# A feed-forward stage in Winograd form: who forms the sums, and in which order the engines' instructions stand

## The chip, the cores and the metric

The program runs on one core of one Trainium2 chip. Its metric is the device time of one execution in microseconds (us). Work is done by five engines, each of which takes its own instructions in their order: TensorE (PE; its weight loads are shown apart as PEld), VectorE (DVE), ScalarE (ACT), GpSimd (POOL) and SyncE (SP). SP issues plain transfers here, POOL issues those that add to what lies at the destination.

## The reference, cut to what matters

Two layers; each is a feed-forward part, a mix of three token mixers, and a second feed-forward part. The change touches the feed-forward parts alone, of which there are four:

```python
def swiglu(h, w_in, w_out):
    gate, up = jnp.split(h @ w_in, 2, axis=-1)
    return (jax.nn.silu(gate) * up) @ w_out
...
    x = x + 0.5 * swiglu(rms_norm(x, ffn1_norm[l]), ffn1_w_in[l], ffn1_w_out[l])
...
    x = x + 0.5 * swiglu(rms_norm(x, ffn2_norm[l]), ffn2_w_in[l], ffn2_w_out[l])
```

x is 512 tokens by 1024 features in float32, w_in 1024 by 5632, w_out 2816 by 1024.

## The kernel before, in words

Every float32 operand is split into a high and a low half of type fp32r (`hi` is a cast on ScalarE, `lo` the difference on VectorE), and a product is three matmuls: high by high, high by low, low by high (`mm3`, lines 214, 218 and 219).

Each feed-forward part has three stretches. The first columns of w_in (six of 22 blocks of 128, four in one part) are multiplied plainly in `cover`, which hides the norm and the preparation of x. The bulk runs in `halved`, a Winograd scheme: a 2-by-2 block product with seven products in place of eight, for which sums of quarters of the weights and of the other operand have to be formed. The last six blocks of w_out are multiplied plainly behind it. The bulk is here called a **stage**; there are four in the trace.

A stage is a list `seq` of products. ("I", w, p) is product p of one unit of w_in (two blocks of columns); ("O", (c, g), p) is product p of one unit of w_out (chunk c of eight hidden blocks, half g). Three stages have 84 products, one has 91. One product is 24 matmuls of 128x256 (two column blocks, four row blocks, three matmuls). While products of later I units run, the O units of the chunk that is complete run between them, in a pattern such as "IIO".

Around each place n of `seq` (here: a **slot**) `halved` emits, through `run(n)`, what later products need:

- `load` (line 568): one quarter of a unit's weights, 512 KB, by an SP transfer into one of eight buffers, four slots before its first use.
- `add` (line 572), `add_second` (line 575) and `add_hidden` (line 623): POOL transfers that add 512 KB from memory, from `S`, or from another quarter of the hidden values `hq`. The sums of an I unit are called S1 (quarter 2 plus quarter 3), S2 (that plus quarter 0), S3 (quarter 0 plus quarter 2) and S4 (quarter 1 plus S2). Before the change S1, S3 and S4 are such transfers, and S2 is a VectorE sum (`second`, line 579). In O units all sums of weights are transfers. The four sums of hidden quarters for each chunk are transfers too.
- `moving` (lines 611 to 620): splits a sum of hidden quarters into halves.
- `prepare` (by `parted`, lines 202 and 203): splits the weights of product n + `LEAD` (2) into a buffer `hl`, of which there are three.

Behind a product come its readings of PSUM: VectorE adds an O product to xT (line 731); for I products ScalarE copies (lines 736, 743, 746) and VectorE adds (739, 749, 752), and the last product of a unit makes hidden values (lines 455, 459, or y in lines 766 to 772).

The order in which the instructions of one engine stand is set by the framework's scheduler, which is free to move an instruction ahead of others that were emitted earlier, as far as dependences allow. `follow` ties an instruction behind the one given to it before on the same engine; before the change only the opening uses it.

Of the kernel before, what the change touches and what calls it, by code (L numbers as in the profile page):

```python
# [32 lines left out]

ORDER_IN = ("P1", "P2", "P6", "P5", "P7", "P3", "P4")
ORDER_OUT = ("P2", "P1", "P5", "P6", "P7", "P3", "P4")
LEAD = 2
# [11 lines left out]
F_Q, F_K, F_V, F_F = 1792, 2304, 2816, 3328  # L48


class Trunk:
# [105 lines left out]
    def act(self, out, in_, func, **kw):  # L157
        i = self.nc.scalar.activation(out, in_, func, **kw)
        if self.tab is not None:
            self.tc.add_manual_dep(i.ins, self.tab, NOSYNC, reason="table order")  # L160
        self.tab_users.append(i.ins.name)

    def follow(self, engine, i):

        if engine in self.chain:
            self.tc.add_manual_dep(i.ins, self.chain[engine], NOSYNC, reason="opening order")
        self.chain[engine] = i.ins.name
# [41 lines left out]
    def mm3(self, acc, ah, al, bh, bl, first, last, parted=False):  # L209

        nc = self.nc
        n = bh.shape[-1]
        for c in (slice(0, n // 2), slice(n // 2, n)) if parted else (slice(0, n),):
            nc.tensor.matmul(  # L214
                acc[:, c], ah, bh[:, c], start=first and c.start == 0, stop=False,
                skip_group_check=True,
            )
        nc.tensor.matmul(acc, ah, bl, start=False, stop=False, skip_group_check=True)  # L218
        nc.tensor.matmul(acc, al, bh, start=False, stop=last, skip_group_check=True)  # L219
# [232 lines left out]
    def hidden(self, out, g, u, other):  # L452

        if other:
            self.nc.vector.scalar_tensor_tensor(
                out=out, in0=g, scalar=-1.0, in1=u, op0=ALU.mult, op1=ALU.mult
            )
        else:
            self.nc.vector.tensor_mul(out, g, u)
# [62 lines left out]
    def halved(self, fp, w_in, w_out, covered):  # L522
# [14 lines left out]
        H = T // 2  # L537

        into = lambda c: [
            ("I", f, p) for f in range(max(covered, c[0]), c[0] + c[1], 2) for p in ORDER_IN  # L540
        ]
        outof = lambda c: [("O", (c, g), p) for p in ORDER_OUT for g in range(2)]
        seq = into(CHUNKS[0])
        for c, pattern in ((0, "IIIO" + "IIO" * 12 + "IO"), (1, "IIIO" + "IOIIO" * 6 + "O")):
            ii, oo = iter(into(CHUNKS[c + 1])), iter(outof(c))
            seq += [next(ii if k == "I" else oo) for k in pattern]
            assert next(ii, None) is None and next(oo, None) is None
        at = {s: n for n, s in enumerate(seq)}

        raw, sums, parts, mov = {}, {}, {}, {}  # L550
        first = covered
        todo = {}

        def when(n, rank, fn, *args):
            todo.setdefault(max(n, -1), []).append((rank, fn, args))

# [9 lines left out]
        def load(u, q, tag):  # L566
            raw[u, q] = t = self.res.tile([P, 4, 2 * P], F32, tag=f"x{tag}", name=self.n("w"))
            nc.sync.dma_start(t, src(u, q))

        def add(u, q, q2):  # L570

            nc.gpsimd.dma_start(raw[u, q], src(u, q2), accum_op=ALU.add)  # L572

        def add_second(u):
            nc.gpsimd.dma_start(raw[u, 1], sums[u], accum_op=ALU.add)

        def second(u):
            sums[u] = t = fp.tile([P, 4, 2 * P], F32, tag="S", name=self.n("S"), bufs=2)
            nc.vector.tensor_add(t, raw[u, 2], raw[u, 0])  # L579

        def at_once(u, name):

            a, b, c, op = {
                1: lambda: (raw[u, 2], raw[u, 2], raw[u, 3], ALU.add),
                3: lambda: (raw[u, 0], sums[u], raw[u, 3], ALU.subtract),
                4: lambda: (raw[u, 1], raw[u, 1], sums[u], ALU.add),
            }[name]()
            nc.vector.tensor_tensor(a, b, c, op=op)

        def prepare(kind, w, p):  # L590
# [9 lines left out]
        SUM = {  # L600
            "P2": (1, 0), "P1": (0, 0), "P5": (0, 0), "P6": (0, 0), "P7": (0, 1),
            "P3": (1, 1), "P4": (0, 0),
        }

        def moving(c, p):
# [5 lines left out]
            if p in ("P1", "P7", "P4"):  # L611
                nc.scalar.activation(hi, t, AF.Copy, scale=-1.0)
                nc.vector.scalar_tensor_tensor(
                    out=lo, in0=t, scalar=-1.0, in1=hi, op0=ALU.mult, op1=ALU.subtract
                )
            else:
                nc.scalar.copy(hi, t)
                nc.vector.tensor_sub(lo, t, hi)
# [6 lines left out]
        lives = []  # L625
        units = list(dict.fromkeys((k, w) for k, w, _ in seq))
        for u in units:
            kind, w = u
            split = {p: at[kind, w, p] - LEAD for p in ORDER_IN}
            if kind == "I":  # L630
                end = {0: "P7", 1: "P3", 2: "P5", 3: "P4"}
                m = split["P6"] - 1
                begin = {
                    0: split["P1"] - AHEAD_LOAD, 1: split["P2"] - AHEAD_LOAD,
                    2: m - AHEAD_SUM - AHEAD_LOAD + 1, 3: split["P4"] - AHEAD_LOAD,
                }
                if w == first:
                    begin = {0: -4, 1: -3, 2: -2, 3: -1}
                    when(0, 0, at_once, u, 1)
                    when(0, 0, second, u)  # L640
                    when(split["P7"] - 1, 2, at_once, u, 3)
                    when(split["P3"] - 1, 2, at_once, u, 4)
                else:
                    when(m - AHEAD_SUM, 5, add, u, 2, 3)
                    when(m, 2, second, u)
                    when(max(m, split["P1"]), 5, add, u, 0, 2)
                    when(max(m, split["P2"]), 6, add_second, u)
            else:
                end = {0: "P7", 1: "P2", 2: "P3", 3: "P4"}
                begin = {  # L650
                    0: split["P1"] - AHEAD_LOAD, 1: split["P2"] - AHEAD_LOAD,
                    2: split["P5"] - AHEAD_SUM - AHEAD_LOAD + 1, 3: split["P4"] - AHEAD_LOAD,
                }
                when(split["P5"] - AHEAD_SUM, 5, add, u, 2, 3)
                when(split["P5"] + 1, 5, add, u, 2, 0)
                when(split["P1"] + 1, 5, add, u, 0, 2)
                when(split["P6"] + 1, 5, add, u, 2, 1)
            for q in range(4):
                lives.append((begin[q], split[end[q]], u, q))

        free = {t: -99 + t for t in range(8)}
        for b, e, u, q in sorted(lives, key=lambda x: x[0]):
            t = min(free, key=free.get)
            assert free[t] <= max(b, 0), (u, q, b, free)
            free[t] = e
            when(b, 4, load, u, q, t)
        for c in range(2):
            n0 = {p: at["O", (c, 0), p] for p in ORDER_OUT}
            for p in ORDER_OUT:
                when(n0[p] - (2 if p == "P2" else 3), 3, moving, c, p)  # L670
            when(n0["P1"] - 2, 7, add_hidden, c, (0, 0), (0, 1))
            when(n0["P5"] - 2, 7, add_hidden, c, (0, 0), (1, 1))
            when(n0["P5"] - 1, 7, add_hidden, c, (0, 1), (1, 1))
            when(n0["P6"] - 2, 7, add_hidden, c, (0, 0), (1, 0))

        def product(u, p, bank, start, stop, parted):
            hi, lo = parts.pop((u, p))
            xh, xl = self.xc[p] if u[0] == "I" else mov[u[1][0], p]
            for i in range(2):
                acc, c = bank[:, i * H : (i + 1) * H], slice(i * P, (i + 1) * P)  # L680
                for k in range(4):
# [3 lines left out]
                        parted and i == 0 and k == 0,  # L685
# [9 lines left out]
        def run(n):  # L695
            if n >= 0 and n + LEAD < len(seq):
                when(n, 1, prepare, *seq[n + LEAD])
            for _, fn, args in sorted(todo.pop(n, []), key=lambda x: x[0]):
                fn(*args)

        run(-1)
        for s in seq[:LEAD]:
            prepare(*s)
        yield
        ring = {"I": (self.ntog + 1) % 2, "O": self.ntog % 2}
# [7 lines left out]
        for n, (kind, w, p) in enumerate(seq):  # L713
            run(n)
# [6 lines left out]
            product(u, p, acc, p in new, p in ("P2", "P3", "P4"), n == 0)  # L721
            if kind == "O":
                c, g = w

                for r, b, f in {
# [5 lines left out]
                    nc.vector.scalar_tensor_tensor(  # L731
                        out=xs, in0=pair(acc), scalar=f, in1=xs, op0=ALU.mult, op1=ALU.add
                    )
            elif p == "P1":
                work[u, "g1"] = g1 = tmp("g1")
                nc.scalar.activation(g1, acc, AF.Copy, scale=-1.0)
            elif p == "P2":
                g1 = work[u, "g1"]
                nc.vector.tensor_add(g1, g1, acc)
                self.act(g1, g1, AF.Silu)  # L740
            elif p == "P6":
                work[u, "g2"] = g2 = tmp("g2")
                nc.scalar.activation(g2, acc, AF.Copy, scale=-1.0)  # L743
            elif p == "P5":
                work[u, "u2"] = u2 = tmp("u2")
                nc.scalar.activation(u2, acc, AF.Copy, scale=-1.0)
            elif p == "P7":
                u2 = work[u, "u2"]
                nc.vector.tensor_add(u2, u2, acc)
            elif p == "P3":  # L750
                g2 = work[u, "g2"]
                nc.vector.tensor_add(g2, g2, acc)
                self.act(g2, g2, AF.Silu)
            else:
                g1, g2, u2 = (work[u, x] for x in ("g1", "g2", "u2"))
                c = next(i for i, (f0, nf) in enumerate(CHUNKS) if f0 <= w < f0 + nf)
                if c < 2:
                    a, k = divmod(w - CHUNKS[c][0], 4)
                    for b, g, v in ((1, g2, u2), (0, g1, acc)):
                        self.hidden(  # L760
                            self.quarter(fp, c, a, b)[:, k : k + 2, :], pair(g), pair(v), a != b
                        )
                else:
                    q = (w - CHUNKS[c][0]) // 2
                    y = fp.tile([P, 2, T], F32, tag="S", name=self.n("y"), bufs=2)
                    nc.vector.tensor_mul(y[:, :, H:], pair(g2), pair(u2))
                    nc.vector.tensor_mul(y[:, :, :H], pair(g1), pair(acc))
# [738 lines left out]
```

## Time and profile before

| | us |
|---|---|
| median of three runs (1947.43 to 1953.0) | 1948.43 |
| profiled execution, its own time | 1955.04 |
| its span, first to last instruction | 1953.3 |
| PE busy in the span | 1875.0 (96%) |
| DVE busy | 1404.8 (72%) |
| ACT busy | 1000.8 (51%) |

The four stages lie at 82.3 to 338.1, 696.6 to 952.6, 1029.7 to 1299.4 and 1657.8 to 1912.4 us of the span; the mixes lie between the first and second and between the third and fourth. In rows that group instructions the first part is line, engine, operation, output and inputs; then the count, the busy time in us, the mean of one in ns, and the idle time of the engine just before them with what ended it. A matmul's busy time overlaps the next one's, so a busy PE need not be at its peak; PEclk is the share of the full clock that was granted.

### The profile page before, as it was taken

What the parts mean: (1) busy time and instruction counts of PE and PEld (TensorE: products, weight loads), DVE (VectorE), ACT (ScalarE), POOL (GpSimd) and SP (SyncE); (2) the same over time, 40 slices, a digit from 0 to 9 for tenths busy, and PEclk for the clock granted to TensorE, in tenths of its full rate; (3) what the DMA queues carried; (4) which work ended last, traced back from release to release, by engine and by line L of the source; (5) the groups of instructions that cost most, each with busy time, mean ns of one, the idle gap of its engine ahead of it and who ended that gap; (6) DMA issues with size and microseconds to landing.
All of it is one profiled execution on the core that took longest, in us unless ns stands there. A gap on an engine that the chain in (4) does not pass through costs nothing.

```text
span 1953.3 us, 33198 instructions
## 1 busy us (share of the span) xinstructions
PE 1875.0 (96%) x13384; PEld 1735.3 (89%) x13384; DVE 1404.8 (72%) x2048; ACT 1000.8 (51%) x1483; POOL 239.8 (12%) x239
## 2 busy tenths in 40 slices
PE   8998999999999998999999989999999999989999
PEld 6898999899878798899989989998998778889997
DVE  7964767578787866677677667766868878756773
ACT  4544455464675543455454545545546663544552
POOL 0022120100000012122001221301000000220310
PEclk9999999999999999999999999999999999999999
DMA  5598794332323389889247989923323234897972
GB/s 140 173 213 176 177 236 106 76 97 71 74 80 103 96 209 198 167 211 220 67 140 169 220 175 213 219 80 76 93 60 88 82 97 144 206 186 180 213 151 87
DMA packets 265658, 281.79 MB, mean 144 GB/s; under 512 B 20608, under 2 KB 246912, under 8 KB 265504
## 3 DMA queue, kind: packets, MB, share of 16 engines
q1 hardware_dynamic: 191792, 183.69, 31.5%
q0 software_dynamic: 73712, 95.97, 30.0%
q8 instruction: 105, 1.72, 0.4%
q14 instruction: 49, 0.40, 0.1%
HBM read 240.23 MB, written 2.10 MB: 124 GB/s over the span
## 4 chain that ended last, share of the span: by engine, by line
PE 67%; DVE 13%; DMA 11%; issue 5%; ACT 4%; POOL 0%; SPq 0%; DVEq 0%; ACTq 0%; POOLq 0%
PE mm L214 10%; PE mm L219 10%; PE mm L218 10%; DMA w<-in_ffn_w_in_dram 7%; DVE hl L203 4%; PE sc L219 4%; PE sc L214 4%; PE sc L218 4%; PE pt L219 4%; PE pt L214 4%; PE pt L218 4%; DMA hq<-hq 3%; PE po L219 3%; PE po L214 2%; PE po L218 2%
## 5 line engine op out<-in xcount | busy, mean ns | idle before, releaser
L202 ACT CAST hl<-w 128x1024 fp32r<-128x1024 f32 x310 | 324.1, 1047 | 345.1 <-PE pt L219 80.9
L203 DVE TENSOR_TENSOR hl<-w,hl 128x1024 fp32r<-128x1024 f32 x310 | 378.4, 1222 | 135.8 <-ACT hl L202 135.7
L219 PE MATMUL mm<-xc,hl 128*128 128x256 f32 x1008 | 281.3, 279 | 1.5 <-DVE hl L203 1.4
L214 PE MATMUL mm<-xc,hl 128*128 128x256 f32 (+1 forms) x1011 | 281.6, 279 | 0.8 <-ACT g L743 0.8
L218 PE MATMUL mm<-xc,hl 128*128 128x256 f32 x1008 | 281.2, 279 | 0.0
L203 DVE TENSOR_TENSOR hl<-st,hl 128x512 fp32r<-128x512 f32 (+2 forms) x204 | 176.2, 865 | 114.6 <-ACT hl L202 113.5
L202 ACT CAST hl<-st 128x512 fp32r<-128x512 f32 (+2 forms) x204 | 155.0, 762 | 186.8 <-PE mm L219 64.5
L214 PEld LDWEIGHTS mm<-xc,hl 128*128 128x128 f32 x1011 | 191.6, 190 | 1.4 <-ACT g L743 1.2
L219 PEld LDWEIGHTS mm<-xc,hl 128*128 128x128 f32 x1008 | 190.1, 189 | 2.3 <-DVE hl L203 2.3
L218 PEld LDWEIGHTS mm<-xc,hl 128*128 128x128 f32 x1008 | 190.8, 189 | 0.0
L572 POOL DMA_DIRECT2D w<-in_ffn_w_in_dram x58 | 76.6, 1340 | 802.5 <-DVE hl L203 350.0
L219 PE MATMUL po<-xc,hl 128*128 128x256 f32 x336 | 98.6, 293 | 23.3 <-DVE hl L203 23.3
L579 DVE TENSOR_TENSOR S<-w,w 128x1024 f32<-128x1024 f32 x33 | 40.4, 1223 | 105.6 <-DMA w<-in_ffn_w_in_dram 105.4
L219 PE MATMUL sc<-m,hl 128*128 128x256 f32 x336 | 98.2, 292 | 18.7 <-DVE hl L203 18.7
L214 PE MATMUL mm<-hl,x 128*128 128x256 f32 (+1 forms) x384 | 112.2, 292 | 0.7 <-DVE ft L304 0.4
L572 POOL DMA_DIRECT2D w<-in_ffn_w_out_dram x64 | 86.7, 1397 | 196.5 <-DVE hl L203 138.9
L214 PE MATMUL mm<-x,hl 128*128 128x512 f32 x272 | 109.4, 402 | 0.0
L219 PE MATMUL mm<-hl,x 128*128 128x256 f32 (+1 forms) x384 | 107.4, 280 | 0.0
L218 PE MATMUL mm<-hl,x 128*128 128x256 f32 (+1 forms) x384 | 107.1, 279 | 0.0
L219 PE MATMUL mm<-x,hl 128*128 128x512 f32 x272 | 106.5, 392 | 0.0
L218 PE MATMUL mm<-x,hl 128*128 128x512 f32 x272 | 106.0, 390 | 0.0
L218 PE MATMUL po<-xc,hl 128*128 128x256 f32 x336 | 97.4, 290 | 0.0
(474 smaller groups left out, 5645.1 us busy)
## 6 DMA issues: line engine op xcount, KB each, us to landing
w<-in_ffn_w_in_dram SPq DMA_DIRECT2D x132, 512.0 KB, 5.3
w<-in_ffn_w_out_dram SPq DMA_DIRECT2D x64, 512.0 KB, 4.6
w<-in_ffn_w_out_dram POOLq DMA_DIRECT2D x64, 512.0 KB, 8.9
w<-in_ffn_w_in_dram POOLq DMA_DIRECT2D x58, 512.0 KB, 7.8
st<-in_ffn_w_in_dram SPq DMA_DIRECT2D x88, 256.0 KB, 3.2
st<-in_w_mix_in_dram SPq DMA_DIRECT2D x88, 256.0 KB, 2.8
hq<-hq POOLq DMA_DIRECT2D x32, 512.0 KB, 9.4
w<-S POOLq DMA_DIRECT2D x29, 512.0 KB, 9.2
```

The source lines that it names most:

```text
L202: a = nc.scalar.copy(hi, src[:, c : c + w])
L203: b = nc.vector.tensor_sub(lo, src[:, c : c + w], hi)
L214: nc.tensor.matmul(acc[:, c], ah, bh[:, c], start=first and c.start == 0, stop=False, skip_group_check=True,)
L218: nc.tensor.matmul(acc, ah, bl, start=False, stop=False, skip_group_check=True)
L219: nc.tensor.matmul(acc, al, bh, start=False, stop=last, skip_group_check=True)
L572: nc.gpsimd.dma_start(raw[u, q], src(u, q2), accum_op=ALU.add)
L579: nc.vector.tensor_add(t, raw[u, 2], raw[u, 0])
```

## The change

Four things in one edit, all in `halved`.

1. **Sums.** For I units S3 becomes a VectorE instruction (S1 and S4 stay transfers). For O units of the first chunk the second sum becomes a VectorE instruction. All sums of hidden quarters become VectorE instructions. In the whole program 69 POOL transfers go and 69 VectorE sums of 128x1024 come.
2. **Order.** Nearly all instructions of a stage on ACT, DVE, POOL and SP, and the first and last matmul of every `mm3`, are tied by `follow` in the order in which they are emitted.
3. **Places.** A new function `plan` sets for each slot what is emitted behind its product. Sums and splits of moving operands that have a choice of slots go to the slot with the least VectorE load. With m the slot in front of the split for P6, S1 is issued in slot m - 5 (m - 4 before), and S2 stands in slot m - 1 or m.
4. **Lead.** `LEAD` goes from 2 to 3, and the preparation is emitted behind the product of its slot instead of ahead of the next one; `hl` still has three buffers. The patterns that interleave I and O products start with one more I product.

```diff
-LEAD = 2
+LEAD = 3
...
+            else:
+                begin[2] = m - 1 - AHEAD_SUM - AHEAD_LOAD
+                begin[3] = split["P7"] - 2 - AHEAD_LOAD
+                when(m - 1 - AHEAD_SUM, 5, "add", u, 2, 3)
+                between(m - 1, m, "total", u, "S2")
+                when(max(m, split["P2"]), 6, "adds", u)
+                between(max(m, split["P1"]) + 1, split["P7"] - 1, "total", u, "S3")
...
+            when(split["P5"] - AHEAD_SUM, 5, "add", u, 2, 3)
+            if w[0]:
+                when(split["P5"] + 1, 5, "add", u, 2, 0)
+            else:
+                between(split["P5"] + 1, split["P5"] + 2, "total", u, "S2")
+            when(split["P5"] + 3, 5, "add", u, 0, 2)
+            when(split["P6"] + 1, 5, "add", u, 2, 1)
...
+        between(n0["P1"], n0["P5"] - 4, "hidden", c, (0, 0), (0, 1))
...
+    for a, b, what in sorted(loose, key=lambda x: (x[1], x[0])):
...
+        n = min(range(a, max(a, b) + 1), key=lambda n: (load[n], n))
+        load[n] += 1024
...
+        A, V, G, S = (lambda i, e=e: self.follow(e, i) for e in "avgs")
...
-            nc.sync.dma_start(t, src(u, q))
+            S(nc.sync.dma_start(t, src(u, q)))
...
-            nc.vector.tensor_add(t, raw[u, 2], raw[u, 0])
...
+            V(nc.vector.tensor_tensor(t, a, b, op=op))
...
-            hi, lo = self.parted(t.rearrange("p k c -> p (k c)"), skew=SKEW_HELD)
+            A(nc.scalar.copy(hi, src))
+            return lambda: V(nc.vector.tensor_sub(lo, src, hi))
...
-        def add_hidden(c, x, y):
+        def total_hidden(c, x, y):
             x, y = (self.quarter(fp, c, *q) for q in (x, y))
-            nc.gpsimd.dma_start(x, y, accum_op=ALU.add)
+            V(nc.vector.tensor_add(x, x, y))
...
         for n, (kind, w, p) in enumerate(seq):
-            run(n)
...
             product(u, p, acc, p in new, p in ("P2", "P3", "P4"), n == 0)
+            rest = prepare(*seq[n + LEAD]) if n + LEAD < len(seq) else None
...
+            if rest is not None:
+                rest()
...
+            run(n)
```

The readings of PSUM between `rest = ...` and `rest()` are the old ones, each now tied in `A` or `V`. So behind product n stand, on VectorE: its reading of PSUM, the low half for product n + 3, then the sums and moving splits of the slot.

More of the change, by code (lines that the diff above doesn't have):

```diff
@@ L48, with plan, when, between @@
 F_Q, F_K, F_V, F_F = 1792, 2304, 2816, 3328
+SUM = {
+    "P2": (1, 0), "P1": (0, 0), "P5": (0, 0), "P6": (0, 0), "P7": (0, 1), "P3": (1, 1), "P4": (0, 0),
+}
+def plan(covered):
+    into = lambda c: [
+        ("I", f, p) for f in range(max(covered, c[0]), c[0] + c[1], 2) for p in ORDER_IN
+    ]
+    outof = lambda c: [("O", (c, g), p) for p in ORDER_OUT for g in range(2)]
+    seq = into(CHUNKS[0])
+    for c, pattern in ((0, "IIIIO" + "IIO" * 11 + "IOIO"), (1, "IIIIO" + "IOIIO" * 5 + "IOIOO")):
+        ii, oo = iter(into(CHUNKS[c + 1])), iter(outof(c))
+        seq += [next(ii if k == "I" else oo) for k in pattern]
+        assert next(ii, None) is None and next(oo, None) is None
+    at = {s: n for n, s in enumerate(seq)}
+    N = len(seq)
+    todo, lives, loose = {n: [] for n in range(-1, N)}, [], []
+    def when(n, rank, *what):
+        todo[max(n, -1)].append((rank, what))
+    def between(a, b, *what):
+        loose.append((max(a, 0), max(b, 0), what))
+    load = [
+        1024 + (
+            512 if kind == "O" else {"P2": 512, "P7": 512, "P3": 512}.get(p, 0) if p != "P4"
+            else 1024 if w < CHUNKS[2][0] else 2048
+        )
+        for kind, w, p in seq
+    ]
+    for u in dict.fromkeys((k, w) for k, w, _ in seq):
+        kind, w = u
+        split = {p: at[kind, w, p] - LEAD for p in ORDER_IN}
+        begin = {0: split["P1"] - AHEAD_LOAD, 1: split["P2"] - AHEAD_LOAD, 3: split["P4"] - AHEAD_LOAD}
+        if kind == "I":
+            end = {0: "P7", 1: "P3", 2: "P5", 3: "P4"}
+            m = split["P6"] - 1
+            if w == covered:
+                begin = {0: -5, 1: -4, 2: -3, 3: -2}
+                when(-1, 9, "total", u, "S1")
+                when(-1, 9, "total", u, "S2")
+                when(0, 2, "total", u, "S3")
+                when(1, 2, "total", u, "S4")
+            else:
[6 more added lines that the diff above has]
+        else:
+            end = {0: "P7", 1: "P2", 2: "P3", 3: "P4"}
+            begin[2] = split["P5"] - AHEAD_SUM - AHEAD_LOAD
+            when(split["P5"] - AHEAD_SUM, 5, "add", u, 2, 3)
+            if w[0]:
+                when(split["P5"] + 1, 5, "add", u, 2, 0)
+            else:
+                between(split["P5"] + 1, split["P5"] + 2, "total", u, "S2")
+            when(split["P5"] + 3, 5, "add", u, 0, 2)
+            when(split["P6"] + 1, 5, "add", u, 2, 1)
+        for q in range(4):
+            lives.append((begin[q], split[end[q]], u, q))
+    free = {t: -99 + t for t in range(8)}
+    for b, e, u, q in sorted(lives, key=lambda x: x[0]):
+        t = min(free, key=free.get)
+        assert free[t] <= max(b, 0) + 2, (u, q, b, free)
+        b, free[t] = max(b, free[t]) if free[t] >= 0 else b, e
+        when(b, 4 if b >= 0 else b - 99, "load", u, q, t)
+    for c in range(2):
+        n0 = {p: at["O", (c, 0), p] for p in ORDER_OUT}
+        last = at["I", CHUNKS[c + 1][0] + (4, 2)[c], "P4"] - 1
+        place = {}
+        for i, p in enumerate(ORDER_OUT):
+            a = at["O", (c, 1), ORDER_OUT[i - 2]] if i > 1 else n0["P2"] - 3
+            loose.append((a, min(n0[p] - 3, last if p == "P7" else N), ("moving", c, p)))
+        between(n0["P1"], n0["P5"] - 4, "hidden", c, (0, 0), (0, 1))
+        between(n0["P5"], n0["P6"] - 4, "hidden", c, (0, 0), (1, 1))
+        between(n0["P6"] - 4, min(n0["P7"] - 4, last - 1), "hidden", c, (0, 1), (1, 1))
+        between(n0["P6"] - 3, min(n0["P4"] - 4, last), "hidden", c, (0, 0), (1, 0))
+    done = {}
+    for a, b, what in sorted(loose, key=lambda x: (x[1], x[0])):
+        key = what[1] if what[0] in ("moving", "hidden") else None
+        a = max(a, done.get(key, 0)) if key is not None else a
+        n = min(range(a, max(a, b) + 1), key=lambda n: (load[n], n))
+        assert n <= max(b, 0), (a, b, what)
+        load[n] += 1024
+        if key is not None:
+            done[key] = n
+        when(n, 3, *what)
+    return seq, {
+        n: [(w[0], w[1:]) for _, w in sorted(todo[n], key=lambda x: x[0])] for n in todo
+    }
@@ L161, in act @@
         self.tab_users.append(i.ins.name)
+        return i
     def follow(self, engine, i):
         if engine in self.chain:
-            self.tc.add_manual_dep(i.ins, self.chain[engine], NOSYNC, reason="opening order")
+            self.tc.add_manual_dep(i.ins, self.chain[engine], NOSYNC, reason="given order")
         self.chain[engine] = i.ins.name
@@ L207, in parted, with mm3 @@
         return hh, ll
-    def mm3(self, acc, ah, al, bh, bl, first, last, parted=False):
+    def mm3(self, acc, ah, al, bh, bl, first, last, parted=False, keep=False):
         nc = self.nc
@@ L217, in mm3 @@
             )
+            if keep:
+                self.follow("p", i)
         nc.tensor.matmul(acc, ah, bl, start=False, stop=False, skip_group_check=True)
-        nc.tensor.matmul(acc, al, bh, start=False, stop=last, skip_group_check=True)
+        i = nc.tensor.matmul(acc, al, bh, start=False, stop=last, skip_group_check=True)
+        if keep:
+            self.follow("p", i)
     def stream(self, *args, **kw):
@@ L537, in halved @@
         H = T // 2
[L539 to L548, printed above, removed]
+        seq, steps = plan(covered)
+        A, V, G, S = (lambda i, e=e: self.follow(e, i) for e in "avgs")
         raw, sums, parts, mov = {}, {}, {}, {}
[L551 to L555, printed above, removed]
         def src(u, q):
@@ L567, in load, with total @@
             raw[u, q] = t = self.res.tile([P, 4, 2 * P], F32, tag=f"x{tag}", name=self.n("w"))
[L568 removed]
+            S(nc.sync.dma_start(t, src(u, q)))
         def add(u, q, q2):
[L572 to L586, printed above, removed]
+            G(nc.gpsimd.dma_start(raw[u, q], src(u, q2), accum_op=ALU.add))
+        def total(u, name):
+            q = lambda i: raw[u, i]
+            if name == "S2" and u[0] == "I":
+                sums[u] = fp.tile([P, 4, 2 * P], F32, tag="S", name=self.n("S"), bufs=2)
+            t, a, b, op = {
+                "S1": lambda: (q(2), q(2), q(3), ALU.add),
+                "S2": lambda: (sums.get(u, q(2)), q(2), q(0), ALU.add),
+                "S3": lambda: (q(0), sums[u], q(3), ALU.subtract),
+                "S4": lambda: (q(1), q(1), sums[u], ALU.add),
             }[name]()
[L588 removed]
+            V(nc.vector.tensor_tensor(t, a, b, op=op))
         def prepare(kind, w, p):
@@ L619, in moving @@
+                V(nc.vector.tensor_sub(lo, t, hi))
             mov[c, p] = hi, lo
-        def add_hidden(c, x, y):
+        def total_hidden(c, x, y):
             x, y = (self.quarter(fp, c, *q) for q in (x, y))
-            nc.gpsimd.dma_start(x, y, accum_op=ALU.add)
[L625 to L674, printed above, removed]
+            V(nc.vector.tensor_add(x, x, y))
@@ L676, in product, with add_second @@
+        def add_second(u):
+            G(nc.gpsimd.dma_start(raw[u, 1], sums[u], accum_op=ALU.add))
+        do = {
+            "load": load, "add": add, "adds": add_second, "total": total, "moving": moving,
+            "hidden": total_hidden,
+        }
         def product(u, p, bank, start, stop, parted):
@@ L695, in run @@
         def run(n):
[L696 to L699, printed above, removed]
+            for name, args in steps[n]:
+                do[name](*args)
+        first = [x for x in steps[-1] if x[0] == "total"]
+        steps[-1] = [x for x in steps[-1] if x[0] != "total"]
         run(-1)
-        for s in seq[:LEAD]:
-            prepare(*s)
+        for s in seq[: LEAD - 1]:
+            prepare(*s)()
         yield
+        for _, args in first:
+            total(*args)
+        prepare(*seq[LEAD - 1])()
         ring = {"I": (self.ntog + 1) % 2, "O": self.ntog % 2}
```

58 lines of the change are left out of this document (28 added, 30 removed).

## The prediction

> **What bounds the kernel now.** I read the page first, then the windows of the four stages, the waits, the transfers, and VectorE's order of time around stalls.
>
> ```profile
> span 1953.3 us, 33198 instructions
> PE 67%; DVE 13%; DMA 11%; issue 5%; ACT 4%; POOL 0%; SPq 0%; DVEq 0%; ACTq 0%; POOLq 0%
> ```
>
> The chain that ended last is TensorE for 67%, but VectorE and transfers hold 24% of it. The windows say where; the columns behind the length are the busy time and count of PE, PEld, DVE, ACT and POOL, then granted clock, DMA share and GB/s. The first four rows are the stages, the next four single stretches of 25 us.
>
> ```profile
> 82.30:338.10 255.80, 238.66 (x2020) 237.44 (x2019) 178.10 (x187) 127.01 (x144) 50.87 (x44) 0.96 0.84 181
> 696.60:952.60 256.00, 243.43 (x2019) 242.39 (x2018) 177.49 (x186) 126.84 (x144) 50.85 (x44) 0.97 0.84 181
> 1029.70:1299.40 269.70, 257.50 (x2188) 256.50 (x2187) 190.51 (x200) 136.87 (x156) 54.36 (x47) 0.98 0.86 186
> 1657.80:1912.40 254.60, 240.00 (x2019) 238.97 (x2018) 177.38 (x186) 125.51 (x143) 50.92 (x44) 0.98 0.85 182
> 225.00:250.00 25.00, 25.00 (x223) 25.00 (x222) 18.53 (x20) 13.88 (x16) 4.36 (x4) 1.00 0.91 204
> 825.00:850.00 25.00, 25.00 (x214) 25.00 (x214) 17.52 (x19) 11.97 (x14) 0.00 (x0) 1.00 0.76 203
> 725.00:750.00 25.00, 22.65 (x182) 22.46 (x181) 15.30 (x17) 10.18 (x12) 7.44 (x7) 0.93 0.99 228
> 1125.00:1150.00 25.00, 23.66 (x207) 23.45 (x206) 18.08 (x20) 12.73 (x15) 6.05 (x5) 1.00 1.01 198
> ```
>
> In 225 to 250 nothing stalls: 223 matmuls touch 25 us, and one takes 0.28 us, so they start every (25 + 0.28)/223 = 0.1134 us. A product of 24 is 2.72 us; that is a slot. Three stages of 84 products and one of 91 are 343 x 2.72 = 933 us. They took 255.8 + 256.0 + 269.7 + 254.6 = 1036.1. So 103 us, 5.3% of the kernel, are above TensorE's own pace, in three parts. PE was idle for 1036.1 - 979.6 = 56.5. The clock was below full for 0.04 x 255.8 + 0.03 x 256.0 + 0.02 x 269.7 + 0.02 x 254.6 = 28.4 us' worth. The rest, 18, is a slower pace without stall: in 825 to 850 one matmul starts every 25.28/214 = 0.1181 us, 4% later; I do not know what sets it.
>
> ```profile
> PE po L219 <- DVE hl L203: 23.3, 6, 4.7
> PE sc L219 <- DVE hl L203: 18.9, 5, 5.8
> PE pt L219 <- DVE hl L203: 7.8, 2, 4.9
> DVE S L579 <- DMA w<-in_ffn_w_in_dram: 105.4, 24, 8.4
> ACT m L617 <- DMA hq<-hq: 13.0, 4, 3.7
> ```
>
> PE's idle time is 13 waits for a low half of weights (50 us of the 56.5). VectorE, which makes them, waited 105.4 us in 24 pieces in front of S2 for a transfer. This is one such piece, and the chain at another kind:
>
> ```profile
> 108.72 1.23 DVE L203 TENSOR_TENSOR hl<-w,hl 128x1024 fp32r<-128x1024 f32 x1 [0.20 <-ACT hl L202]
> 117.51 1.23 DVE L579 TENSOR_TENSOR S<-w,w 128x1024 f32<-128x1024 f32 x1 [7.57 <-DMA w<-in_ffn_w_in_dram]
> 118.65 1.22 DVE L203 TENSOR_TENSOR hl<-w,hl 128x1024 fp32r<-128x1024 f32 x1
> ...
> 150.99 0.52 POOL w L572
> 151.52 0.20 issue
> 151.71 10.04 DMA hq<-hq
> 161.76 1.23 DVE hl L203
> ```
>
> At 109.9 VectorE has reached S2 and stands for 7.57 us; the low half that PE wants stands behind it. In the instructions as VectorE got them, this S2 has 12 splits of held weights of the stage in front of it, while the list of steps puts it into slot 17, behind 19: the scheduler moved it 7 splits forward, ahead of its data. The other S2 stand 5, 25, 35, 44, 60 and 72 splits in. The second chain is a hidden sum: issued by POOL behind other transfers, 10.04 us in flight, and a split behind it.
>
> **The change, part by part.**
>
> ```profile
> q0 software_dynamic: 17886, 23.48, 55.8%
> q1 hardware_dynamic: 22420, 22.51, 28.1%
> w<-in_ffn_w_in_dram SPq DMA_DIRECT2D x26, 512.0 KB, 8.5
> w<-in_ffn_w_out_dram SPq DMA_DIRECT2D x16, 512.0 KB, 4.9
> w<-in_ffn_w_out_dram POOLq DMA_DIRECT2D x16, 512.0 KB, 8.7
> w<-in_ffn_w_in_dram POOLq DMA_DIRECT2D x13, 512.0 KB, 7.8
> hq<-hq POOLq DMA_DIRECT2D x8, 512.0 KB, 10.0
> w<-S POOLq DMA_DIRECT2D x7, 512.0 KB, 8.7
> L579 DVE TENSOR_TENSOR S<-w,w 128x1024 f32<-128x1024 f32 x33 | 40.4, 1223 | 105.6 <-DMA w<-in_ffn_w_in_dram 105.4
> L203 DVE TENSOR_TENSOR hl<-w,hl 128x1024 fp32r<-128x1024 f32 x310 | 378.4, 1222 | 135.8 <-ACT hl L202 135.7
> L731 DVE SCALAR_TENSOR_TENSOR xT<-pt,xT 128x512 f32<-128x512 f32 x14 | 9.6, 689 | 1.6 <-PE pt L219 1.6
> ```
>
> (The first stage's transfers with counts, KB and median us to landing; then VectorE groups.)
>
> *Transfers removed.* 44 adding transfers of the first stage hold 55.8% of the 16 DMA engines for 255.8 us: 3.24 us each. Its 42 loads of weights and one tail load hold 28.1%: 1.67 each. The change takes away 8 hidden sums, 7 S3 and 2 sums of O units: 17, or 55 us. With 28 adds (one is issued ahead of the window) and 43 loads the engines need 28 x 3.24 + 43 x 1.67 = 163 us of a 228 us stage, 0.71 where 0.84 was. Landings should come down from 7.8 to 10.0 towards 6 to 8.
>
> *Sums added.* 17 x 1.22 = 21 us of VectorE for a stage, 69 x 1.22 = 84 in all, 178 + 21 = 199 of 228 us (87%). None is free if VectorE falls behind, so I added up each slot: 1.22 for the split, 0.69 for a reading of PSUM (two at a unit's last product, and there the split of y in the last chunk), 1.22 for each sum or moving split. The worst run is slots 65 to 70: 3.13 + 3.12 + 3.12 + 3.13 + 3.81 + 3.13 = 19.4 where six slots are 16.3, so 3.1 us behind. A split is the second instruction of its slot and its product starts two slots later: 2 x 2.72 - 0.69 - 1.22 = 3.5 us of room. Elsewhere the backlog stays under 2.4. So the sums lie beside TensorE's work, with 0.4 us to spare at one place; without that cover they would cost up to their 84.
>
> *Order.* S2 may no longer be moved forward: the seven now stand behind 8, 18, 29, 39, 50, 62 and 74 splits, 2 to 6 slots (5 to 16 us) later than 5, 12, 25, 35, 44, 60 and 72. The longest wait was 8.4. S1 is issued 4 or 5 slots, 10.9 to 13.6 us, ahead of S2; landing takes 7.8 at the median: no wait left, with 3 us over. The hidden sums' waits go with the transfers; behind them the next split would be late only from VectorE's own backlog. What the tie adds: a sum that waits holds every PSUM reading and split behind it on VectorE, and PE after 3.5 us; on POOL an add whose operand is late holds the next adds; on SP a load that waits for its buffer holds the next loads, which have 3 to 5 slots to their first use.
>
> *Lead.* LEAD 3 with three buffers: the split for n + 3 needs the buffer of product n, which is free when product n ends, where before the split for n + 2 stood ahead of product n and waited for n - 1. The same two slots of room; I take 0, bounds -2 and +2 us a stage (the opening, where VectorE is busy without a gap with the last plain columns).
>
> *Where transfers still crowd.* Slots 53 to 70 carry 12 adds and 8 loads: 12 x 3.24 + 8 x 1.67 = 52 us in 18 x 2.72 = 49. They run up to 3 us late there, against margins of 1.5 to 3. I take one residual wait of 2 us of PE a stage; bounds 0 and 5.
>
> *Clock.* The 2.35 us of idle time in 725 to 750 came with a mean clock of 0.93 (1.7 us lost); the 1.34 us in 1125 to 1150 with 1.00. So a rest of 2 us costs its length and at most 1.7 more; I take 0.5 a stage. The Trainium skill (TensorE: Matmul & The Clock Gate, "Why this matters for your kernels") puts the limit at idle gaps of more than about 3 us, so by it the residual wait would cost no clock, 2 us less in all; the row with 2.35 us speaks for a lower limit, and I go by the row.
>
> *The pace.* Which of 0.1134 and 0.1181 holds changes in the trace around stalls. I take the same 18 us; bounds 0 and 933 x 4% = 37.
>
> **Sum** over four stages: idle 56.5 to 8, clock 28.4 to 2, pace 18 to 18: 74.9 us less. From the profiled execution (1955.04; 1.7 outside its span) that is 1880.1. That execution lies 6.6 above the median of the runs, so I forecast 1948.4 - 74.9 = 1873.5. Bounds of the terms: idle and clock to nothing and the best pace, 103 less, 1845; idle 4 x 5, clock 4 x 1.7, the pace throughout slow, 1948.4 - 36.5 - 21.6 + 19 = 1909.
>
> **Rivals.**
>
> *Transfers stay late at part of the sites.* For it: 0.71 is a mean, and slots 53 to 70 ask for more than the engines give; the medians of 7.8 to 10.0 come from such crowds. Then one of three long waits a stage stays, about 5 us and 2.5 of clock: 4 x 7.5 = 30 in place of 10, 1893 (1912 with the slow pace throughout). Against: S2 no longer stands ahead of its data.
>
> *The tie turns slower.* One mechanism: VectorE, in a fixed order, stands at each of the seven S2 of a stage until S1 lands, and cannot make other splits meanwhile. A stage gets slower than before when this costs over 103/4 = 26 us, so 3.7 us at each S2: 2 of idle and 1.7 of clock. PE idles 2 us when VectorE waits 5.5, so S1 would have to land 10.9 + 5.5 = 16 us after its issue. At 5 us of idle and 3.4 of clock each it is 4 x 7 x 8.4 = 235 against 103: 2080; at 4 in all, 1957. Against: medians of 7.8 to 10.0 with more traffic. The Trainium skill (SBUF — State Buffer, "Who interferes with whom") says that a VectorE instruction with two SBUF inputs and a GpSimd instruction that reads SBUF hold each other off; that speaks against 69 more such sums beside POOL's issues. A POOL issue of the old S1 took about 1.3 us in a stage where VectorE ran such sums for most of the time, as shown here:
>
> ```profile
> L572 POOL DMA_DIRECT2D w<-in_ffn_w_in_dram x13 | 16.8, 1326 | 95.1 <-DVE hl L203 74.6 <-DMA w<-in_ffn_w_in_dram 13.6 <-issue 7.0
> ```
>
> If each issue waited for one more sum it would land 1.2 us later, within the 3 over, far from 16.
>
> *Nothing changes.* The new waits of VectorE take just the place of the old, as they would if it were bound by its own work: 199 of 228 us and the 0.4 us of room speak for it, the slots elsewhere against. About 1948.
>
> **Numbers.** Forecast 0.66, late transfers 0.22 (both faster), slower 0.08, no change 0.03; 0.01 is for a gain under the bounds. About 0.3% (6 us) is what a measurement of this kernel can tell from no change. Faster 0.88, same 0.03, slower 0.09. The range, 1848 to 1912, holds the forecast's bounds and most of the late transfers.
>
> **What would show it.** Right: the stages' windows 232 to 240 us long (248 to 258 the long one), PE idle under 4 us in each, clock 0.99 or 1.00, DVE near 199 us, DMA share near 0.70, no hq<-hq issues; waits of the sums for transfers under 20 us in all in place of 105.4. Wrong: PE waits for low halves behind a VectorE without gaps (then the sums are not covered), or long waits of sums for adds in slots 53 to 70 (the crowd), or a clock under 0.98.

## The result, and the profile after

The changed kernel takes 1874.91 us (median of four runs, 1868.1 to 1883.93) where the kernel before takes 1947.93 beside it: a ratio of 0.963, 95% interval 0.957 to 0.969. The profiled execution took 1880.58 us, its span is 1878.8. These are its four stages, in the columns of the table of before (PE, PEld, DVE, ACT, POOL busy, granted clock, DMA share, GB/s):

```profile
81.50:315.80 234.30, 231.88 (x2019) 231.48 (x2018) 197.05 (x204) 126.92 (x144) 32.23 (x27) 0.99 0.69 158
675.10:908.70 233.60, 230.94 (x2020) 230.60 (x2019) 196.26 (x204) 127.40 (x144) 32.16 (x27) 0.99 0.70 160
985.70:1238.60 252.90, 250.19 (x2188) 249.70 (x2187) 210.21 (x218) 137.49 (x156) 34.41 (x29) 0.99 0.69 160
1596.90:1837.80 240.90, 239.03 (x2019) 238.80 (x2018) 195.19 (x202) 126.52 (x143) 32.17 (x27) 0.99 0.67 154
sum 961.70, PE 952.05 PEld 950.58 DVE 798.71 ACT 518.34 POOL 130.97; mean PE 238.01 PEld 237.64 DVE 199.68 ACT 129.58 POOL 32.74
```

The stages take 961.7 us where they took 1036.1; the 74.4 us between them are the whole gain (the spans differ by 74.5). VectorE is busy for 75 us more, POOL for 76 less. Above the 933 us of TensorE's own pace 29 are left: 961.7 - 952.05 = 9.7 idle, the rest clock and pace. The waits (engine, line and who is waited for; us in total, times, longest):

```profile
PE mm L326 <- ACT g L799: 6.9, 3, 2.7
PE sc L326 <- ACT g L799: 2.6, 1, 2.6
ACT hl L697 <- DMA w<-in_ffn_w_in_dram: 9.3, 4, 3.1
ACT hl L697 <- DMA w<-in_ffn_w_out_dram: 5.8, 3, 2.4
DVE w L685 <- DMA w<-in_ffn_w_in_dram: 2.4, 2, 2.0
```

The waits of VectorE in front of S2 (105.4 us before) are gone from the list, and PE's 13 long waits for low halves with them. What stands in their place is one wait in each stage, for a reading of PSUM by ScalarE at line 799. The rows of ScalarE and of TensorE in the first stage show why, and the window around them what it costs (cut where dots stand):

```profile
93.08 1.04 ACT L697 CAST hl<-w 128x1024 fp32r<-128x1024 f32 x1 [2.13 <-DVE w L685]
94.03 0.62 ACT L269 ACTIVATE gi<-gi 128x512 f32<-128x512 f32 x1
94.56 0.58 ACT L799 ACTIVATE g<-mm 128x512 f32<-128x512 f32 x1
...
95.19 0.38 PE L326 MATMUL mm<-xc,hl 128*128 128x256 f32 x1 [2.42 <-ACT g L799]
...
92.00:99.00 7.00, 4.58 (x26) 4.39 (x26) 4.69 (x6) 3.49 (x5) 0.00 (x0) 0.76 0.53 162
```

The first unit's P7 adds to the bank that holds P6, which ScalarE has to read first. That reading is tied behind the cast for P3, and the cast waits 2.13 us for S4, which VectorE forms late because the last plain columns' work is still on it. PE stands for 2.42 us, and the granted clock over these 7 us is 0.76: another 0.24 x 7 = 1.7 us.

### The profile page after: what moved, and what is told of

It reads as the page before. It is cut to its first block, busy times and chain, and to the rows that moved or that the text cites. A ratio compares the mean times of both kernels' runs of the same rounds, so it can differ in the third digit from the quotient of the medians.

```text
span 1878.8 us, 33066 instructions
## 1 busy us (share of the span) xinstructions
PE 1848.1 (98%) x13384; PEld 1711.3 (91%) x13384; DVE 1480.0 (79%) x2117; ACT 1002.6 (53%) x1483; POOL 163.6 (9%) x170
## 5 line engine op out<-in xcount | busy, mean ns | idle before, releaser
L333 PE MATMUL sc<-m,hl 128*128 128x256 f32 x336 | 93.6, 279 | 0.0
L332 PE MATMUL sc<-m,hl 128*128 128x256 f32 x336 | 93.4, 278 | 0.0
L326 PE MATMUL sc<-m,hl 128*128 128x256 f32 x336 | 93.4, 278 | 0.0
L326 PE MATMUL po<-xc,hl 128*128 128x256 f32 x336 | 93.4, 278 | 0.0
L332 PE MATMUL po<-xc,hl 128*128 128x256 f32 x336 | 93.4, 278 | 0.0
L333 PE MATMUL po<-xc,hl 128*128 128x256 f32 x336 | 93.4, 278 | 0.0
```

What stands on the lines that cost most here:

```text
L326: i = nc.tensor.matmul(acc[:, c], ah, bh[:, c], start=first and c.start == 0, stop=False, skip_group_check=True,)
L333: i = nc.tensor.matmul(acc, al, bh, start=False, stop=last, skip_group_check=True)
```

## Experiments

All times are medians; the kernel before took 1953.0 to 1953.4 us beside each of the three lots of experiments and the last one, so times across lots are compared by their ratio to it. The code shown is cut where dots stand. A "hold" is one dependence that fixes one instruction's place.

**1. The changed kernel without its ties.**

```diff
-        A, V, G, S = (lambda i, e=e: self.follow(e, i) for e in "avgs")
+        A = V = G = S = lambda i: i
```

The tie in `product` is left out too.

> The changed kernel with all ties of the stages taken away (sums, places and lead as changed); the scheduler then puts the seven S2 of a stage 5, 10, 25, 35, 44, 60 and 71 splits in, where the tied order has 8, 18, 29, 39, 50, 62 and 74. Theory (S2 ahead of its data is what stalls): waits of VectorE in front of sums come back, over 50 us in all, PE idle 25 to 45 us in the stages, 1900 to 1945 us. Rival (fewer adding transfers suffice, a share of 0.71 lands in time even for an early S2): waits under 20 us, 1865 to 1885 us.

1891.5 us, 0.969 (0.966 to 0.972), between the two forecasts. Waits and the stages' sum:

```profile
DVE S L685 <- DMA w<-in_ffn_w_in_dram: 53.5, 18, 8.7
sum 977.30, PE 955.63 PEld 953.06 DVE 794.61 ACT 520.80 POOL 130.24; mean PE 238.91 PEld 238.26 DVE 198.65 ACT 130.20 POOL 32.56
```

With S2 moved forward the waits in front of it come back, but half of what they were (53.5 of 105.4) and PE idles 21.7 us, less than the 25 I gave as the least. So sums, places and lead together, without the order, take away some 62 of the 78 us that are to be had up to 1875. Which of them does it is not shown: adds to w_in land 8.2 us after their issue at the median here (7.8 before, with S3 among them), no sooner, while the plan issues S1 a slot earlier.

**2. The kernel before, all tied in the order of emission** (sums and places of before, `LEAD` 2).

```diff
+        A, V, G, S = (lambda i, e=e: self.follow(e, i) for e in "avgs")
...
-            nc.vector.tensor_add(t, raw[u, 2], raw[u, 0])
+            V(nc.vector.tensor_add(t, raw[u, 2], raw[u, 0]))
```

> The kernel before, its sums on transfers, its places and its lead of 2, with all instructions of a stage tied in the order in which they are emitted (S2 then 9, 20, 30, 41, 51, 63 and 75 splits in). Theory (order and hidden transfers both matter): S2's waits go, one wait a stage for a hidden transfer and some for crowded adds stay, PE idle 15 to 30 us in the stages, 1890 to 1925 us. Rival (order alone): 1865 to 1885 us. Rival (transfers alone): 1940 to 1955 us, as before.

1931.8 us, 0.990 (0.987 to 0.994): slower than my theory's range. S2's waits are gone, others are not:

```profile
ACT hl L203 <- DMA w<-in_ffn_w_out_dram: 59.7, 17, 6.4
ACT m L622 <- DMA hq<-hq: 20.3, 4, 5.6
DVE S L584 <- DMA w<-in_ffn_w_in_dram: 2.2, 4, 1.1
sum 1009.70, PE 969.10 PEld 954.83 DVE 711.18 ACT 509.92 POOL 208.59; mean PE 242.28 PEld 238.71 DVE 177.80 ACT 127.48 POOL 52.15
```

A given order by itself is worth 22 us: ScalarE now stands at casts of weights whose POOL adds are late, and PE idles 40.6 us where 15 to 30 were expected.

**3. The kernel before with S2 alone held** behind the split that is emitted in front of it.

```diff
-            nc.vector.tensor_add(t, raw[u, 2], raw[u, 0])
+            i = nc.vector.tensor_add(t, raw[u, 2], raw[u, 0])
+            if u[1] != first:
+                self.tc.add_manual_dep(i.ins, self.low, NOSYNC, reason="held")
```

(`self.low` is the last low half emitted.)

> The kernel before with one tie for each S2 alone: behind the split that is emitted in front of it; nothing else is changed. Theory: 9 of the 13 long waits of PE go with their clock, 1880 to 1905 us, and the waits for hidden sums stay. Rival (the transfers' traffic is what is late): the wait moves to other readers of transfers, 1930 to 1955 us.

1890.8 us, 0.968 (0.965 to 0.971): my theory. Some thirty dependences and nothing else bring 62.7 us.

```profile
ACT hl L202 <- DMA w<-in_ffn_w_in_dram: 36.2, 16, 6.8
ACT m L620 <- DMA hq<-hq: 21.6, 6, 5.1
sum 966.50, PE 952.00 PEld 948.64 DVE 720.59 ACT 520.89 POOL 207.70; mean PE 238.00 PEld 237.16 DVE 180.15 ACT 130.22 POOL 51.92
```

No wait in front of S2 is in the list; 14.5 us of idle PE stay. The rival was right in part: ScalarE's casts now wait for w_in (36.2 us; such waits are not in the list of before), and longer for hidden sums (21.6 us, 13.0 before); both are part of the 33 us that stay above TensorE's pace.

**4. The opening's order.** In slots 0 to 3 the readings of PSUM stand ahead of the next cast.

```diff
-            rest = prepare(*seq[n + LEAD]) if n + LEAD < len(seq) else None
+            rest = prepare(*seq[n + LEAD]) if 4 <= n < len(seq) - LEAD else None
...
+            if n < 4:
+                rest = prepare(*seq[n + LEAD])
             if rest is not None:
                 rest()
```

> The changed kernel with one swap: in slots 0 to 3 the readings of PSUM stand ahead of the cast and low half for product n + 3, as ScalarE's reading of P6 stands behind a cast that waits for S4. Theory (the stall of 1.9 to 2.7 us and the half clock of 3.4 us at each stage's opening come from that place in ScalarE's order): both go, about 4 x 4 = 16 us, 1855 to 1866 us, PE idle in the stages under 4 us. Rival (VectorE is the bound of the opening, with the last plain columns' work beside the first unit's): PE then waits for the low half of P3 in place of ScalarE, 1868 to 1884 us.

1864.9 us, 0.955 (0.952 to 0.959), as the theory said; the wait at line 799 is down to 0.2 us, the clock is full and PE idles 3.5 us:

```profile
sum 942.70, PE 939.23 PEld 936.75 DVE 795.42 ACT 516.86 POOL 130.99; mean PE 234.81 PEld 234.19 DVE 198.86 ACT 129.21 POOL 32.75
```

**5. Hidden sums back on transfers**, they and the moving splits in the slots of before; all else as changed.

```diff
-        between(n0["P1"], n0["P5"] - 4, "hidden", c, (0, 0), (0, 1))
...
+        when(n0["P1"] - 2, 7, "hidden", c, (0, 0), (0, 1))
...
-            V(nc.vector.tensor_add(x, x, y))
+            G(nc.gpsimd.dma_start(x, y, accum_op=ALU.add))
```

> The changed kernel with the four hidden sums of each chunk again as POOL transfers, they and the moving splits in the slots of before; all else as changed, tied. 36 adds a stage, a DMA share of about 0.77. Theory (a hidden sum in flight for 9 to 10 us holds the moving split and what is tied behind it): ScalarE waits for hidden transfers again, 20 us or more in all, PE idle 15 to 30 us in the stages, 1890 to 1910 us. Rival (in the new order they land in time): 1866 to 1885 us.

1931.4 us, 0.989 (0.982 to 0.995), worse than my theory's range: in a tied order the hidden transfers cost over 40 us.

```profile
ACT hl L696 <- DMA w<-in_ffn_w_out_dram: 54.1, 11, 8.6
DVE hh L832 <- DMA hq<-hq: 22.5, 4, 5.9
```

Most of the waiting is not for the hidden sums themselves but for adds to O weights. They share POOL's tied queue with the hidden transfers; that these are what makes them late is argued, not shown.

**6. The weights' sums back on transfers** (S3 and the first chunk's second sum); hidden sums stay on VectorE.

```diff
-                between(max(m, split["P1"]) + 1, split["P7"] - 1, "total", u, "S3")
+                when(max(m, split["P1"]), 5, "add", u, 0, 2)
...
-                between(split["P5"] + 1, split["P5"] + 2, "total", u, "S2")
+            when(split["P5"] + 1, 5, "add", u, 2, 0)
```

> The changed kernel with S3 and the first chunk's second sum again as POOL transfers in the slots of before; hidden sums stay on VectorE, all tied. 37 adds a stage, a DMA share of about 0.80, VectorE 11 us a stage less busy. Theory (traffic costs by crowding): waits for adds in the second half of the stages, 1878 to 1900 us. Rival (with S2 in its place the traffic is free): 1866 to 1878 us.

1878.7 us, 0.962 (0.956 to 0.968), on the border of the two forecasts and by its ratio as the changed kernel: the weights' sums that the change moved are worth nothing that these runs can tell. Its stages run at a DMA share of 0.80 to 0.83.

**7. The kernel before with VectorE alone tied.** The edit of 2 with `A`, `G`, `S` and the tie in `product` left out.

> The kernel before with VectorE's instructions of the stages alone tied in the order of emission; ScalarE, POOL, SP and TensorE are free. All tied it took 1931.8 us, with S2 alone held 1890.8. Theory A (VectorE's tie costs: what waits there holds PSUM readings and splits): 1915 to 1935 us. Theory B (the ties of the other engines cost: a late add holds ScalarE's casts and POOL's queue): 1885 to 1900 us.

1940.1 us, 0.994 (0.991 to 0.997): slower than either theory says, A the nearer. ScalarE waits 91.6 us for hidden transfers, 13.0 in the kernel before:

```profile
ACT m L624 <- DMA hq<-hq: 91.6, 13, 10.6
```

**8. The changed kernel with VectorE alone free of ties** (`V = lambda i: i`).

> The changed kernel with VectorE alone free of ties; the scheduler puts S2 5, 11, 26, 36, 45, 60 and 72 splits in. Free on all engines it took 1891.5 us. Theory (VectorE's order carries that difference, by S2's place): 1885 to 1900 us, VectorE waits over 40 us for transfers in front of S2. Rival (the order of the others carries it): 1866 to 1880 us.

1895.3 us, 0.969 (0.962 to 0.975), as with no tie at all; the time is my theory's, the wait 3 us short of it in the profile, which is of the fastest of the four runs (1882.0):

```profile
DVE S L686 <- DMA w<-in_ffn_w_in_dram: 36.8, 14, 4.3
```

So what the given order adds to the rest of the change lies in VectorE's order.

**9. The changed sums without ties, S2 alone held**, and on the same chip the changed kernel and the opening's swap once more.

```diff
-        A, V, G, S = (lambda i, e=e: self.follow(e, i) for e in "avgs")
+        A = V = G = S = lambda i: i
...
+            if name == "S2" and u != ("I", covered):
+                self.tc.add_manual_dep(i.ins, self.low, NOSYNC, reason="held")
```

(`self.low` is again the last low half emitted; the tie in `product` is left out.)

> The changed kernel without its ties, but with each S2 held behind the low half that is emitted in front of it: 8, 18, 29, 39, 50, 62 and 74 splits in, as in the changed kernel; all else is free. Theory (of the order only S2's place matters once the hidden sums are on VectorE): the waits in front of S2 go, the opening's stall is not there, 1860 to 1876 us, at or under the changed kernel. Rival (the whole order is needed): 1885 to 1895 us, as free.

> The changed kernel once more, on the same chip as the opening's swap. 1868 to 1884 us, a stall and a half clock at each stage's opening; if the pace of matmuls is drawn anew at a stall, times lie about 8.5 us apart, a stage each.

> The opening's swap once more, on the same chip as the changed kernel. If it gains what its stages showed, 10 to 16 us under the changed kernel, 1858 to 1870; if the first result was the draw of the pace, within 5 us of it.

S2 held: 1855.7 us, 0.952 (0.948 to 0.956), faster than the theory's range. The changed kernel: 1888.6, 0.968 (0.963 to 0.973), above its forecast. The swap: 1865.2, 0.956 (0.952 to 0.961), as forecast, but 23 us under the changed kernel where 10 to 16 were. All three ran on one chip: the whole order is not needed, and it costs 33 us against the one hold, 23 of which the swap takes back. The stages' sums with S2 held, and of the changed kernel in this profile; then one stretch of the changed kernel in its first profile and in this one:

```profile
sum 936.40, PE 935.48 PEld 934.49 DVE 795.20 ACT 520.89 POOL 130.24; mean PE 233.87 PEld 233.62 DVE 198.80 ACT 130.22 POOL 32.56
...
sum 984.70, PE 975.97 PEld 975.03 DVE 798.80 ACT 519.60 POOL 131.02; mean PE 243.99 PEld 243.76 DVE 199.70 ACT 129.90 POOL 32.75
...
200.00:225.00 25.00, 25.00 (x223) 25.00 (x223) 18.90 (x21) 11.32 (x14) 2.21 (x2) 1.00 0.60 168
200.00:225.00 25.00, 25.00 (x215) 25.00 (x214) 18.66 (x20) 12.22 (x14) 0.30 (x1) 1.00 0.61 179
```

The same kernel, 961.7 and 984.7 us in its stages, with 9.7 and 8.7 us of idle PE: the 23 us between the two profiles are the pace, 223 against 215 matmuls in 25 us at full clock. So is most of what the order costs here: of the 48.3 us between the stages with S2 held and those of the second profile 7.8 are idle PE, some 7 the clock of four openings, and the rest, some 34, the slower pace.

**10. The kernel before with two edits alone**: S2 held as in 3, and the hidden sums on VectorE.

```diff
-            nc.gpsimd.dma_start(x, y, accum_op=ALU.add)
+            nc.vector.tensor_add(x, x, y)
```

> The kernel before with two edits alone: S2 held behind the split in front of it, and the hidden sums on VectorE; the weights' sums stay on transfers, the places and the lead of 2 stay, no other tie. With S2 held alone the rest above TensorE's pace was 33 us in its profile, of which waits for hidden sums and for adds. Theory (hidden transfers make most of that rest, weights' sums on transfers are nearly free): 1855 to 1872 us. Rival (the weights' traffic makes it): 1878 to 1892 us, as with S2 held alone.

1853.3 us (1851.99 to 1860.79), 0.950 (0.946 to 0.954). It beats the kernel before and the changed one; its stages:

```profile
82.30:311.00 228.70, 228.70 (x2019) 228.66 (x2018) 187.25 (x195) 128.34 (x144) 43.96 (x36) 1.00 0.84 184
...
sum 934.10, PE 934.10 PEld 933.95 DVE 756.20 ACT 522.08 POOL 179.12; mean PE 233.53 PEld 233.49 DVE 189.05 ACT 130.52 POOL 44.78
```

PE is never idle, the clock is full, and the sum is the 933 us of TensorE's own pace, with the DMA share that the kernel before had, 0.84.

## Why the prediction was right, and where its steps were not

**The size of what was to be had** was right: 103 us above TensorE's pace were forecast as the most, and experiment 10 reaches it (934.1 of 1036.1). Of the terms, idle 56.5 to 8 came out at 9.7, clock and pace together 46.4 to 20 at about 19. The sum, 74.9, came out at 74.4 in the stages. Within it errors cancel.

**S2 ahead of its data** was the right cause. Its hold alone brings 62.7 us (experiment 3), and wherever S2 moves forward again its waits are back (1 and 8). What S2 waited for was read too narrowly. The wait shown at 117.51 did not end with S1. This is what ended it, as SP's queue issued it and as a piece of the chain:

```profile
107.94 2.39 SPq L568 DMA_DIRECT2D w<-in_ffn_w_in_dram  x2
107.94 9.47 DMA w<-in_ffn_w_in_dram
```

It is a plain load (line 568), so quarter 0: the adds that POOL had issued ahead of it, at 99.75 and 102.99, had landed by 110.6. In the whole trace of before, 9 of the waits, 35 of the 105.4 us, end with such a load and 70 us with an add. S2 stood ahead of both its operands; it also stands behind 20 splits in the emitted order, not 19 (experiment 2).

**"Transfers removed"** had the right amounts (0.67 to 0.70 of the DMA engines where 0.71 was forecast) and a wrong effect. Landings of adds from memory did not come down to 6 to 8 us in the changed kernel (whole program):

```profile
w<-in_ffn_w_out_dram POOLq DMA_DIRECT2D x56, 512.0 KB, 8.4
w<-in_ffn_w_in_dram POOLq DMA_DIRECT2D x29, 512.0 KB, 8.1
w<-S POOLq DMA_DIRECT2D x29, 512.0 KB, 4.8
```

Only those from `S` did, from 9.2. Without the ties the adds to w_out land in 6.4 and 6.3 us (1 and 9), with the same number of transfers; so here it is the order that goes with the longer ones. Nor is the traffic a cost by itself: experiments 6 and 10 run at 0.80 to 0.84 with nothing lost. In experiment 1 the waits of an S2 that comes too early are half as long, but that lighter traffic does this, and not the earlier issue of S1, is not shown. The part of the sums that counts is the hidden ones (5 and 6, and 10 against 3: 37 us by the medians).

**"What the tie adds"** was named and priced at nothing. It is the step that failed most: the tie is what holds S2, but the rest of it costs 33 us in experiment 9 (21 by the ratios, if the first result, 0.963, is put beside S2 held, 0.952), and with hidden transfers in it, it eats most of the gain (2, 5, 7). The step on **lead** took 0 with 2 us each way; the opening lost 2.4 idle and 1.7 clock, outside that bound, at a place that I had named but for VectorE, not for ScalarE's order. In return the 2 us a stage in slots 53 to 70 did not come. Residual and opening swapped places in the sum.

**The clock.** I took 0.5 us a stage and each opening lost 1.7. The page TensorE: Matmul & The Clock Gate of the Trainium skill ("Why this matters for your kernels") has a limit of about 3 us of idle time; in the changed kernel the gaps of 1.87 to 2.66 us at the four openings were each followed by half clock, as the row of before with 2.35 had suggested, and the measurement decides. But the length of the gap does not settle it: in experiment 6 two openings with gaps of 1.87 and 2.57 us kept a clock of 1.00 (685 to 695 and 1002 to 1012 us), and so did the kernel before behind a gap of 3.17 us (1690 to 1700). Which gaps bring the half clock stays open.

**The pace** was carried as 18 with bounds of 0 and 37. The two profiles of the changed kernel have about 12 and 36. It decides more of this kernel's spread than anything else, and that the forecast, 1873.5, came within 2 us of the first median, 1874.9, is luck beside that spread (1868 to 1905 over all its runs).

**The rivals.** S1 never landed 16 us after its issue (11.9 at most in this profile), and VectorE was bound nowhere: the worst run of slots did not stall PE. POOL's issues of S1, all six of the first stage and then two of its issues that follow each other:

```profile
L672 POOL DMA_DIRECT2D w<-in_ffn_w_in_dram x6 | 8.8, 1474 | 15.8 <-DVE hl L699 9.4 <-DMA w<-in_ffn_w_in_dram 6.3
...
105.33 0.90 POOL L722 DMA_DIRECT2D w<-S  x1 [31.08 <-DVE hl L699]
105.88 1.67 POOL L672 DMA_DIRECT2D w<-in_ffn_w_in_dram  x1
```

The mean, 1474 ns, is above the 1326 of before, as the page SBUF — State Buffer of the Trainium skill ("Who interferes with whom"), on VectorE instructions with two SBUF inputs and GpSimd instructions that read SBUF, could have it. The single issues speak against that here: three of the six start 0.55 us behind an issue from `S` and take 1.66 to 1.67 us, and the other three take 1.28 to 1.29, as S1's issues before (1.28 to 1.30 where they start alone). The sums cost POOL nothing that these rows show.

## What to carry to other kernels

Where an in-order engine stands at a transfer, compare the place of that instruction in the engine's order with the place where its data are due, before making the transfer cheaper: holding one instruction did here about as much (0.968) as moved sums, a planner and a full order together (0.963 and 0.968), and with the hidden sums on VectorE it did more (0.950). A full order cures what a scheduler put too early and makes every late operand hold all that stands behind it, so hold the few that wait for transfers and leave the rest free. A transfer that produces an operand for the next step in the same chain (the hidden sums) was better done here by the engine that waits for it; one whose consumer is several slots away could stay a transfer.

## What the runs showed of the hardware

The matmul stream has two paces at full clock, 0.1134 and 0.118 us for the same instructions, and stays in one for hundreds of matmuls. In the profiles without a long wait (experiments 9 and 10) every stage ran at the faster one; in the second profile of the changed kernel all four went over to the slower at the opening's stall and stayed there. Most changes of pace lie at a stall, but a stall is not needed: in the first stage of the first profile 223 matmuls start in 260 to 285 us and 214 in 290 to 315, with TensorE never idle. What sets the pace stays open, and so does whether the stall is what brings the slower one. And DMA engines that are busy for 0.84 of a stage, with adds that land 6.9 to 9.0 us after their issue at the median (experiment 10), cost nothing there.
